# Down projection of a gated MLP as seven block products per pair of channel tiles

## The chip, the cores and the metric

The kernel runs on one core of a Trainium2 chip. A core has five engines with a queue each: TensorE (PE, with its weight loads as PEld), VectorE (DVE), ScalarE (ACT), GpSimd (POOL) and SyncE (SP), which here issues the transfers. The metric is the device time of one execution in microseconds.

## What is computed

```python
def _conv_ffn(x, w_up, conv_f_w, conv_f_b, w_down):
    h = _causal_depthwise_conv(x @ w_up, conv_f_w, conv_f_b)
    gate, val = h[..., :D_FF], h[..., D_FF:]
    return (jax.nn.silu(gate) * val) @ w_down

def reference(...):
    mix = _token_mixing(x, w_in, b_in, ...)
    x = _layernorm(DEEPNORM_ALPHA * x + mix, ln1_g, ln1_b)
    ffn = _conv_ffn(x, w_up, conv_f_w, conv_f_b, w_down)
    return _layernorm(DEEPNORM_ALPHA * x + ffn, ln2_g, ln2_b)
```

x is 1024 x 1024 in float32, D_FF is 2816, which is 22 tiles of 128 channels. The change lies in the product with w_down (2816 x 1024) and the last norm.

## The kernel before

Every float32 operand is split (`split`, L73 to L80) into a rounded high part, a cast on ACT at L75, and a low part, a subtract at L78 on POOL or DVE; three matmuls (high x high, high x low, low x high) make one product.

The program has four parts. The first computes the token mixing, the first norm and x1, which is kept in DRAM (`x1d`). The second runs the up units, one per tile f of 128 channels (`unit`, L702). A unit makes the gate tile `upg` and the value tile `upv`, 128 x 1024 each in PSUM, by a form of Strassen's scheme: seven products of 12 matmuls of 128x512 each in place of eight. Its weights are the row sums `sa` and `sb`, four DVE subtracts or adds (L692, L693, L696, L698 in `prep_unit`, for the unit after), split on ACT and POOL into `ws`, `wa`, `wb`, `wd`. Three DVE adds (L720, L721, L714) put the products' parts together in PSUM; the product t1 of the following unit goes to a half of the gate tile that L714 has read. Then the causal convolution of width 3 follows (`conv3`, ACT L633 and DVE L636), silu (L644), gate x value (L650 on DVE), and the result, `cg`, is stored to DRAM as `hd[f]` (L652).

The third is the down part. For each half of the rows (th) and each f, `down_prep` loads w_down[f] (`dr`) and half of hd[f] (`hr`), and splits them: `dh`, `dl` on ACT and POOL, `ho` on ACT and DVE. `down_step` then makes 6 matmuls for each of the four row tiles s of that half, into one 128x1024 PSUM tile `pd` per row tile, which collects over all f. The last, `finish`, adds ALPHA x1, takes the statistics (`rstd_row`, L98), and scales by g2 and b2: partly on ACT, POOL and DVE, row tile 7 in three pieces on DVE.

The order of the work is the order of the program for each queue, as the scheduler puts it; tiles of a pool wait until an older tile of the same tag is read to its end. The pools that matter are `raw` (3 buffers, loads to be split), `A` and `B` (16 each, split operands) and the PSUM pools `mm`, `un` and `dn`.

```python
            for n in range(2, 2 * NF):
                th, f = n // NF, n % NF
                ahead(n + 2)
                for s in range(4 * th, 4 * th + 4):
                    down_step(s, f)
```

## Time and profile before

| | |
|---|---|
| median of 3 runs | 997.17 us (995.89 to 997.5) |
| the profiled execution | 996.77 us |
| its span | 994.7 us, 2.07 us less than its time |
| PE busy | 964.9 us, 97% |
| DVE busy | 664.7 us, 67% |
| POOL busy | 534.9 us, 54% |
| ACT busy | 444.8 us, 45% |
| granted PE clock, mean | 0.993 |

The clock is a share of 2.4 GHz. Up to about 366 us the first part and the first unit run, from there to 741 us the other up units, to 985 us the down part, and then the end. "us from the start" counts from the start of the span. A row of the timeline gives start, length, engine, line, operation, output <- inputs, and in brackets the idle time before it with what released it. Numbers of buffers are left out of names, so `ws` stands for four split sums of a unit.

### The profile page before, as it was taken

To read this page: it belongs to the slowest core of one execution; us is meant where nothing else is said; L and a number is where in the kernel's file an instruction comes from. 1 tells how busy PE (TensorE), PEld (TensorE's weight loads), DVE (VectorE), ACT (ScalarE), POOL (GpSimd) and SP (SyncE) were. 2 spreads that over 40 slices of the span, in tenths; PEclk is the share of its full clock that TensorE was granted. 3 is DMA by queue.
4 is the path that set the end of the run, shared out by engine and by line. 5 is a ranking of instruction groups with operands and counts; after the bars stand their busy time and mean duration, and the time that the engine had idled before them with its cause. 6 is when DMAs were issued, how large, how long until landed. Compare 5 with 4: busy or idle time off the path is not lost.

```text
span 994.7 us, 11745 instructions
## 1 busy us (share of the span) xinstructions
PE 964.9 (97%) x4344; PEld 796.5 (80%) x4344; DVE 664.7 (67%) x890; ACT 444.8 (45%) x661; POOL 534.9 (54%) x341
## 2 busy tenths in 40 slices
PE   8999999999997799999999999999999999999996
PEld 6888888878885678888888888888877888888885
DVE  4699999987499995675675576567378344680007
ACT  5233864763634554454454444445455423343202
POOL 4245944775835974454544445445518744489402
PEclk9999999999998999999999999999999999999999
DMA  8111131321420233123123112212458744336102
GB/s 323 64 43 43 43 106 43 122 70 43 166 110 21 76 119 106 72 84 106 64 69 116 70 64 101 90 65 85 170 189 301 251 147 156 133 107 219 54 0 85
DMA packets 33177, 106.84 MB, mean 107 GB/s; under 512 B 3680, under 2 KB 4064, under 8 KB 33120
## 3 DMA queue, kind: packets, MB, share of 16 engines
q1 hardware_dynamic: 33120, 106.09, 30.3%
q8 instruction: 34, 0.56, 0.2%
q14 instruction: 23, 0.19, 0.1%
HBM read 86.16 MB, written 19.92 MB: 107 GB/s over the span
## 4 chain that ended last, share of the span: by engine, by line
PE 76%; DVE 17%; ACT 3%; DMA 2%; issue 1%; SPq 0%; POOL 0%; DVEq 0%; ACTq 0%
PE pd L828 23%; PE upv L624 20%; PE upg L624 15%; PE ps L215 8%; PE po L537 8%; DVE acc L263 6%; DMA xraw<-in_xT 1%; DVE cg L636 1%; DVE tq L758 1%; DVE tq L757 1%; DMA dr<-in_w_down 1%; DVE wol L78 1%; DVE ast L351 1%; DVE sa L693 1%; ACT vt L363 1%
## 5 line engine op out<-in xcount | busy, mean ns | idle before, releaser
L828 PE MATMUL pd<-dh,ho 128*128 128x512 f32 x688 | 213.4, 391 | 0.7 <-ACT dh L75 0.7
L78 POOL TENSOR_TENSOR dl<-dr,dh 128x1024 fp32r<-128x1024 f32 x44 | 109.8, 2507 | 87.8 <-ACT dh L75 87.8
L828 PEld LDWEIGHTS pd<-dh,ho 128*128 128x128 f32 x688 | 130.0, 189 | 28.0 <-ACT dh L75 1.1
L828 PE MATMUL pd<-dl,ho 128*128 128x512 f32 x344 | 134.7, 392 | 1.7 <-POOL dl L78 1.7
L263 DVE SCALAR_TENSOR_TENSOR acc<-ybin,cv,acc 128x512 f32<-128x512 f32 x196 | 134.2, 744 | 0.9 <-ACT acc L257 0.3
L78 DVE TENSOR_TENSOR ho<-hr,ho 128x512 fp32r<-128x512 f32 x44 | 77.8, 1790 | 61.2 <-ACT ho L75 61.2
L78 POOL TENSOR_TENSOR ws<-sb,ws 128x512 fp32r<-128x512 f32 x42 | 55.5, 1321 | 79.9 <-ACT ws L75 79.9
L75 ACT CAST dh<-dr 128x1024 fp32r<-128x1024 f32 x44 | 46.2, 1051 | 109.1 <-issue 50.3
L828 PEld LDWEIGHTS pd<-dl,ho 128*128 128x128 f32 x344 | 64.9, 189 | 15.7 <-POOL dl L78 2.2
L720 DVE TENSOR_TENSOR upv<-upv,pb 128x512 f32<-128x512 f32 x21 | 14.7, 698 | 78.9 <-PE upv L624 78.9
L78 POOL TENSOR_TENSOR ws<-sa,ws 128x512 fp32r<-128x512 f32 x42 | 58.9, 1405 | 6.1 <-ACT ws L75 6.1
L78 POOL TENSOR_TENSOR wa<-ur,wa 128x512 fp32r<-128x512 f32 x21 | 27.3, 1300 | 62.2 <-ACT wa L75 59.9
L636 DVE SCALAR_TENSOR_TENSOR cg<-upg,cv,cg 128x1023 f32<-128x1023 f32 (+4 forms) x46 | 56.6, 1230 | 5.9 <-ACT cg L633 5.3
L624 PE MATMUL upg<-b21h,wb 128*128 128x512 f32 x168 | 58.1, 391 | 1.6 <-POOL wb L78 1.2
L75 ACT CAST ws<-sb 128x512 fp32r<-128x512 f32 x42 | 26.1, 622 | 72.6 <-PE upv L624 70.3
L624 PE MATMUL upv<-b11h,wa 128*128 128x512 f32 x168 | 55.4, 391 | 2.1 <-DVE cg L636 2.1
L636 DVE SCALAR_TENSOR_TENSOR cv<-upv,cv,cv 128x1023 f32<-128x1023 f32 (+4 forms) x46 | 56.6, 1230 | 1.1 <-ACT cv L633 0.5
L624 PE MATMUL upv<-t2h,ws 128*128 128x512 f32 x168 | 55.3, 390 | 1.9 <-ACT pa L712 1.9
L624 PE MATMUL upg<-t1h,ws 128*128 128x512 f32 x168 | 55.3, 390 | 0.0
L624 PE MATMUL upv<-t4h,wd 128*128 128x512 f32 x168 | 55.3, 390 | 0.0
L624 PE MATMUL upv<-t3h,ws 128*128 128x512 f32 x168 | 55.1, 389 | 0.0
L624 PE MATMUL upg<-b22h,ws 128*128 128x512 f32 x168 | 55.1, 389 | 0.0
(411 smaller groups left out, 2340.0 us busy)
## 6 DMA issues: line engine op xcount, KB each, us to landing
ur<-in_w_up SPq DMA_DIRECT2D x44, 512.0 KB, 3.4
dr<-in_w_down SPq DMA_DIRECT2D x44, 512.0 KB, 3.9
hd<-cg SPq DMA_DIRECT2D x22, 512.0 KB, 2.9
hr<-hd SPq DMA_DIRECT2D x44, 256.0 KB, 3.2
wr<-in_w_in SPq DMA_DIRECT2D x14, 512.0 KB, 3.3
xres<-in_x SPq DMA_DIRECT2D x8, 512.0 KB, 3.9
wor<-in_w_out SPq DMA_DIRECT2D x8, 512.0 KB, 3.3
x1d<-xres SPq DMA_DIRECT2D x8, 512.0 KB, 2.6
```

Of the source, the lines that this page charges most:

```text
L75: nc.scalar.copy(hi, raw)
L78: lo_eng.tensor_tensor(out=lo, in0=raw, in1=hi.bitcast(F32), op=ALU.subtract)
L215: nc.tensor.matmul(ps[hf] if isinstance(ps, list) else ps[:, ts(hf, 512)], wt[:, ts(k, P)], xt(k, hf), start=first and k == 0, stop=(not f ...
L263: nc.vector.scalar_tensor_tensor(out=xs(0) if k == 0 else acc, in0=xs(k), scalar=w(k), in1=first if n == 0 else acc, op0=ALU.mult, op1=ALU ...
L351: nc.vector.bn_stats(st[:, n * 8 + g * 4 + c], tp[:, c])
L363: nc.scalar.activation(vc, vc, AF.Identity, bias=nb[:, i : i + 1], scale=r[:, i : i + 1])
L537: nc.tensor.matmul(po[:, ts(hf, 512)], a, b[:, ts(hf, 512)], start=first and i == 0, stop=last and i == 2)
L624: nc.tensor.matmul(out, w[a][:, ts(k, P)], x[b][k // 2][:, k % 2], start=first and k == 0 and i == 0, stop=last and k == 3 and i == 2, ski ...
L636: nc.vector.scalar_tensor_tensor(out=c[:, o:b], in0=ps[:, o - sh : b - sh], scalar=w(k), in1=c[:, o:b], op0=ALU.mult, op1=ALU.add,)
L693: tt(out=s2, in0=s1, in1=a11, op=ALU.subtract)
L720: v(out=w22, in0=x, in1=p5, op=ALU.add)
L828: nc.tensor.matmul(pd, hh[f][a][:, ts(s % 4, P)], wd[f][b][:, c0:c1], start=first and i == 0, stop=last and i == 2,)
```

## The change

Pairs of row tiles (p and p+4, p from 0 to 3), pairs of channel tiles (kp, 11 of them) and the two halves of the columns make 2 x 2 block products; each is now done with seven products in place of eight, of 3 matmuls each. The sums on the side of w_down do not depend on the hidden layer. `sum_prep(kp)` makes them in 11 of the up units: it loads two tiles of w_down (`dq0`, `dq1`), takes four DVE subtracts of 128x512 (L806 to L809), splits the result on ACT and POOL, and stores the four parts to DRAM. `wop_prep` loads these again in the down part, and splits the plain blocks. `hop_prep` loads parts of hd for a pair of row pairs, makes the sums with four DVE operations (L860 to L863) and splits all on ACT and POOL. `step` runs one product of a row pair, over one or two kp, into one half of one of two PSUM tiles, `xy0` and `xy1`; product 2 collects in a bank of its own (`z`) over all kp. After products 1, 6, 5, 3, 7 and 4 `accum` adds half a tile into x1 in SBUF (L927; the first time L930 with ALPHA). The order of products of a block is the string `seq`; the blocks take their kp in the order of `blocks`, so that the last four each finish one row pair. All row tiles but the last are then scaled on ACT and twice on POOL (L977 and L978).

```diff
-    ) as ap_, tc.tile_pool(name="b", bufs=16) as bp, tc.tile_pool(name="raw", bufs=3) as rawp, tc.tile_pool(
+    ) as ap_, tc.tile_pool(name="b", bufs=16) as bp, tc.tile_pool(name="raw", bufs=6) as rawp, tc.tile_pool(
...
-        def down_prep(th, f):
...
+        blocks = [
+            ((2, 3), (0,)), ((0, 1), (0, 1)), ((2, 3), (1, 2)), ((0, 1), (2, 3)), ((2, 3), (3, 4)), ((0, 1), (4, 5)),
+            ((2, 3), (5, 6)), ((0, 1), (6, 7)), ((2, 3), (7, 8)), ((0, 1), (8,)),
+        ] + [((p,), (9, 10)) for p in (0, 1, 2, 3)]
+
+        def sum_prep(kp):
+            w0, w1 = (load(w_down[2 * kp + i], f"dq{i}_{kp}") for i in range(2))
+            tt = nc.vector.tensor_tensor
+            b11, b12, b21, b22 = w0[:, 0:512], w0[:, 512:1024], w1[:, 0:512], w1[:, 512:1024]
+            tt(out=b11, in0=b12, in1=b11, op=ALU.subtract)
+            tt(out=b12, in0=b22, in1=b12, op=ALU.subtract)
+            tt(out=b22, in0=b22, in1=b11, op=ALU.subtract)
+            tt(out=b21, in0=b21, in1=b22, op=ALU.subtract)
+            wsum[kp] = []
+            for i, w in enumerate((w0, w1)):
+                hi = rawp.tile([P, 1024], F32R, tag="raw", name=f"dsh{i}_{kp}")
+                lo = w.bitcast(F32R)
+                split(w, hi, lo, nc.scalar, nc.gpsimd)
+                for q, t in (("h", hi), ("l", lo)):
+                    d = dp.tile([P, 1024], F32, name=f"ds{q}{i}_{kp}")
+                    nc.sync.dma_start(d, t.bitcast(F32))
+                    wsum[kp].append(d)
+
+        def wop_prep(kp):
+            ops = []
+            for i, d in enumerate(wsum[kp]):
+                t = A(F32R, f"ds{kp}_{i}")
+                nc.sync.dma_start(t.bitcast(F32), d)
+                ops.append((t[:, 0:512], t[:, 512:1024]))
+            b0 = rawp.tile([P, 512], F32, tag="raw", name=f"db0_{kp}")
+            nc.sync.dma_start(b0, w_down[2 * kp][:, 0:512])
+            b1 = load(w_down[2 * kp + 1], f"db1_{kp}")
+            h0 = A(F32R, f"dh0_{kp}", (P, 2, 512))
+            split(b0, h0[:, 0], h0[:, 1], nc.scalar, nc.gpsimd)
+            if kp % 3 == 2:
+                h1, l1 = (bp.tile([P, 1024], F32R, tag="B", name=f"d{q}1_{kp}") for q in "hl")
+            else:
+                h1, l1 = (wp.tile([P, 1024], F32R, tag=f"w{q}", name=f"d{q[0]}1_{kp}", bufs=2) for q in ("hi", "lo"))
+            split(b1, h1, l1, nc.scalar, nc.gpsimd)
+            (t1h, t3h), (t1l, t3l), (t4h, t2h), (t4l, t2l) = ops
+            wops[kp] = {
+                1: (h0[:, 0], h0[:, 1]), 2: (h1[:, 0:512], l1[:, 0:512]), 3: (h1[:, 512:1024], l1[:, 512:1024]),
+                5: (t1h, t1l), 6: (t2h, t2l), 7: (t3h, t3l), 4: (t4h, t4l),
+            }
+
+        def hop_prep(n):
+            pairs_, ks = blocks[n]
+            c0 = pairs_[0] // 2 * 256
+            nk = len(ks)
+            raw = []
+            for i in range(2):
+                t = rawp.tile([P, 2, nk, 256], F32, tag="raw", name=f"hr{n}_{i}")
+                for j, kp in enumerate(ks):
+                    nc.sync.dma_start(
+                        t[:, :, j], hd[2 * kp + i].rearrange("p (m c) -> p m c", m=2)[:, :, c0 : c0 + 256]
+                    )
+                raw.append(t)
+            a11, a21, a12, a22 = raw[0][:, 0], raw[0][:, 1], raw[1][:, 0], raw[1][:, 1]
+            ss = [rawp.tile([P, 2, nk, 256], F32, tag="raw", name=f"hs{n}_{i}") for i in range(2)]
+            s1, s2, s4 = ss[0][:, 0], ss[0][:, 1], ss[1][:, 0]
+            tt = nc.vector.tensor_tensor
+            tt(out=s1, in0=a21, in1=a22, op=ALU.add)
+            tt(out=a21, in0=a11, in1=a21, op=ALU.subtract)
+            tt(out=s2, in0=s1, in1=a11, op=ALU.subtract)
+            tt(out=s4, in0=a12, in1=s2, op=ALU.subtract)
+            op = lambda q: bp.tile([P, 2, nk, 256], F32R, tag="B", name=f"ho{n}_{q}")
+            o = [op(i) for i in range(7)]
+            split(raw[0], o[0], o[1], nc.scalar, nc.gpsimd)
+            split(raw[1], o[2], o[3], nc.scalar, nc.gpsimd)
+            split(ss[0], o[4], o[5], nc.scalar, nc.gpsimd)
+            split(s4, o[6][:, 0], o[6][:, 1], nc.scalar, nc.gpsimd)
...
+                for kp in range(NP):
+                    if 2 + kp * 9 // 5 == f:
+                        sum_prep(kp)
                 if f == NF - 1:
-                    for n in range(3):
-                        down_prep(0, n)
+                    down_prep(0)
+                    for t in (2, 6, 3, 7, 0, 4, 1, 5):
+                        load_x1(t)
+                    down_prep(1)
                 value_tile(f, gate_tile(f))
...
-            def down_mm(pd, s, f, c0, c1, first, last):
...
+            def down_prod(bank, n, ks, q, j, first, last):
+                for i, kp in enumerate(ks):
+                    for c, (a, b) in enumerate(((0, 0), (0, 1), (1, 0))):
+                        nc.tensor.matmul(
+                            bank, hops[n][q][a][:, i, ts(j, P)], wops[kp][q][b],
+                            start=first and i == 0 and c == 0, stop=last and i == len(ks) - 1 and c == 2,
+                            skip_group_check=True,
+                        )
+
+            def accum(bank, s, hf, out=None):
+                dst = xr_[s][:, ts(hf, 512)]
+                if (s, hf) in touched:
+                    nc.vector.tensor_tensor(out=dst if out is None else out, in0=bank, in1=dst, op=ALU.add)
+                else:
+                    touched.add((s, hf))
+                    nc.vector.scalar_tensor_tensor(out=dst, in0=dst, scalar=ALPHA, in1=bank, op0=ALU.mult, op1=ALU.add)
+
+            def step(n, q, i):
+                pairs_, ks = blocks[n]
+                p = pairs_[i]
+                b = xy[p % 2]
+                x, y = b[:, 0:512], b[:, 512:1024]
+                j = p % 2
+                end = n == len(blocks) - 1
+                if q == 2:
+                    if p not in zs:
+                        zs[p] = dnp.tile([P, 512], F32, tag="dn", name=f"z{p}")
+                    fin = ks[-1] == NP - 1
+                    down_prod(zs[p], n, ks, 2, j, p not in zused, fin)
+                    zused.add(p)
+                    if fin:
+                        accum(zs[p], p, 0)
+                    return
+                down_prod(y if q in (5, 3) else x, n, ks, q, j, q in (1, 5), q in (4, 3))
+                if q == 1:
+                    accum(x, p, 0)
+                if q == 6:
+                    accum(x, p, 1)
+                if q == 5:
+                    accum(y, p + 4, 1)
+                if q == 3:
+                    accum(y, p, 1)
+                if q == 7:
+                    accum(x, p + 4, 1, y if end else None)
+                if q == 4:
+                    accum(x, p + 4, 0, x if end else None)
+
+            def finish(s):
+                t = xr_[s]
+                mv = stats(s, [t[:, ts(hf, 512)] for hf in range(2)])
+                r, nb = rstd_row(mv, f"l2_{s}", True)
+                cuts = [(0, 512), (512, 1024)] if s == 3 else [(0, 1024)]
+                for a, b in cuts:
+                    nc.scalar.activation(t[:, a:b], t[:, a:b], AF.Identity, bias=nb, scale=r)
+                    nc.gpsimd.tensor_tensor(out=t[:, a:b], in0=t[:, a:b], in1=g2[:, a:b], op=ALU.mult)
+                    nc.gpsimd.tensor_tensor(out=t[:, a:b], in0=t[:, a:b], in1=b2[:, a:b], op=ALU.add)
+                    nc.sync.dma_start(out[s][:, a:b], t[:, a:b])
...
+            for n, (pairs_, ks) in enumerate(blocks):
+                if n + 1 < len(blocks):
+                    down_prep(n + 1)
+                if len(pairs_) == 2:
+                    seq = "1a1b5a5b6a6b7a7b3a3b4a4b2a2b" if n == 0 else "1a1b2a2b6a6b5a5b7a7b3a4a4b3b"
+                else:
+                    seq = "1a5a6a3a7a2a4a"
+                for q, i in zip(seq[0::2], seq[1::2]):
+                    step(n, int(q), "ab".index(i))
+                if ks[-1] == NP - 1:
+                    p = pairs_[0]
+                    finish(p)
+                    if n < len(blocks) - 1:
+                        finish(p + 4)
                     else:
+                        finish_last(p + 4, [xy[p % 2][:, ts(hf, 512)] for hf in range(2)])
 
 
 def kernel(**inputs):
```

The order of DVE's instructions beside up unit 11, before. The names carry the unit's number; `upv11` is its value tile, `sa14` the row sums made for a later unit, `upg12` the gate tile that the next t1 waits for (its L714 is the ninth row):

```order
L720 TENSOR_TENSOR upv11_4342<-upv11_4342,pb11_4348 128x512
L692 TENSOR_TENSOR sa14_4713<-ur14_1_4619 128x512
L721 TENSOR_TENSOR upg11_4341<-upg11_4341,pa11_4347 128x512
L693 TENSOR_TENSOR sa14_4713<-sa14_4713,ur14_0_4617 128x512
L696 TENSOR_TENSOR sb14_4714<-ur14_0_4617,ur14_1_4619 128x512
L698 TENSOR_TENSOR sb14_4714<-ur14_0_4617,sa14_4713 128x512
L636 SCALAR_TENSOR_TENSOR cg11_4466<-upg11_4341,cv_84,cg11_4466 128x1023
L636 SCALAR_TENSOR_TENSOR cg11_4466<-upg11_4341,cv_84,cg11_4466 128x1022
L714 TENSOR_TENSOR upg12_4478<-upg12_4478,pa12_4484 128x512
L636 SCALAR_TENSOR_TENSOR cv11_4471<-upv11_4342,cv_84,cv11_4471 128x1023
L636 SCALAR_TENSOR_TENSOR cv11_4471<-upv11_4342,cv_84,cv11_4471 128x1022
```

and after, where pair 5 has its sums:

```order
L806 TENSOR_TENSOR dq0_5_4576<-dq0_5_4576 128x512
L720 TENSOR_TENSOR upv11_4452<-upv11_4452,pb11_4458 128x512
L807 TENSOR_TENSOR dq0_5_4576<-dq1_5_4578,dq0_5_4576 128x512
L808 TENSOR_TENSOR dq1_5_4578<-dq1_5_4578,dq0_5_4576 128x512
L692 TENSOR_TENSOR sa14_4867<-ur14_1_4773 128x512
L809 TENSOR_TENSOR dq1_5_4578<-dq1_5_4578 128x512
L721 TENSOR_TENSOR upg11_4451<-upg11_4451,pa11_4457 128x512
L693 TENSOR_TENSOR sa14_4867<-sa14_4867,ur14_0_4771 128x512
L696 TENSOR_TENSOR sb14_4868<-ur14_0_4771,ur14_1_4773 128x512
L698 TENSOR_TENSOR sb14_4868<-ur14_0_4771,sa14_4867 128x512
L636 SCALAR_TENSOR_TENSOR cg11_4598<-upg11_4451,cv_84,cg11_4598 128x1023
L714 TENSOR_TENSOR upg12_4610<-upg12_4610,pa12_4616 128x512
```

The first `dq0` subtract (L806) stands ahead of L720, and the other three between L720 and L721. L714 stands behind one of the two conv adds in place of both.

POOL's order at the same place, after. Before, `ws4`, `wd`, `wb` and `wa` follow one another there without the `dq` rows:

```order
L78 TENSOR_TENSOR ws412_4570<-sb12_4550,ws412_4570 128x512
L78 TENSOR_TENSOR dq0_5_4576<-dq0_5_4576,dsh0_5_4584 128x1024
L78 TENSOR_TENSOR wd12_4573<-ur12_1_4455,wd12_4573 128x512
L78 TENSOR_TENSOR wb13_4713<-ur13_0_4612,wb13_4713 128x512
L78 TENSOR_TENSOR dq1_5_4578<-dq1_5_4578,dsh1_5_4591 128x1024
L78 TENSOR_TENSOR wa13_4710<-ur13_0_4612,wa13_4710 128x512
```

The two 128x1024 `dq` subtracts stand ahead of `wd` and of `wa`.

DVE in a full block of the down part, after (`hs5` are the row sums for the block that follows). Before, DVE had there only one `ho` subtract per half of a hidden tile, with nobody on PE's side waiting between:

```order
L927 TENSOR_TENSOR x1r0_6099<-xy0_6173,x1r0_6099 128x512
L927 TENSOR_TENSOR x1r1_6103<-xy1_6174,x1r1_6103 128x512
L860 TENSOR_TENSOR hs5_0_6684<-hr5_0_6678,hr5_1_6681 128x512
L927 TENSOR_TENSOR x1r0_6099<-xy0_6173,x1r0_6099 128x512
L861 TENSOR_TENSOR hr5_0_6678<-hr5_0_6678 128x512
L862 TENSOR_TENSOR hs5_0_6684<-hs5_0_6684,hr5_0_6678 128x512
L927 TENSOR_TENSOR x1r1_6103<-xy1_6174,x1r1_6103 128x512
L863 TENSOR_TENSOR hs5_1_6685<-hr5_1_6681,hs5_0_6684 128x512
L927 TENSOR_TENSOR x1r4_6101<-xy0_6173,x1r4_6101 128x512
L927 TENSOR_TENSOR x1r5_6105<-xy1_6174,x1r5_6105 128x512
L927 TENSOR_TENSOR x1r4_6101<-xy0_6173,x1r4_6101 128x512
L927 TENSOR_TENSOR x1r5_6105<-xy1_6174,x1r5_6105 128x512
```

Each L927 frees a half of `xy0` or `xy1` for PE's next product on that tile, and the four sums for the next block stand between them. Over the down part PE has 924 matmuls of 128x512, in place of the work of 1056.

## Rows read from the trace of the kernel before

**Rows 1.** windows: span time, then busy us and matmul count of each engine, granted clock, DMA
```profile
core 0: us, PE busy (x) PEld busy (x) DVE busy (x) ACT busy (x) POOL busy (x), PEclk, DMA share, GB/s
366.00:724.00 358.00, 357.44 (x1578) 295.71 (x1577) 220.17 (x219) 165.59 (x244) 178.44 (x132) 1.00 0.26 92
...
748.00:870.00 122.00, 122.00 (x533) 100.85 (x532) 65.51 (x40) 45.53 (x58) 69.65 (x28) 0.99 0.56 195
870.00:985.00 115.00, 115.00 (x519) 95.70 (x518) 38.88 (x64) 27.89 (x35) 59.60 (x24) 1.00 0.26 92
```

**Rows 2.** the chain that ended last, in order of time: the row of the down products
```profile
747.21 232.66 PE pd L828 x1018
```

**Rows 3.** DVE and POOL timelines inside one up unit: start us, us, instruction
```profile
585.93 0.70 DVE L720 TENSOR_TENSOR upv<-upv,pb 128x512 f32<-128x512 f32 x1 [4.21 <-PE upv L624]
...
591.07 1.77 DVE L696 TENSOR_TENSOR sb<-ur,ur 128x512 f32<-128x512 f32 x1 [1.19 <-POOL wd L78]
592.76 0.68 DVE L698 TENSOR_TENSOR sb<-ur,sa 128x512 f32<-128x512 f32 x1
593.36 2.59 DVE L636 SCALAR_TENSOR_TENSOR cg<-upg,cv,cg 128x1023 f32<-128x1023 f32 x2
595.87 0.69 DVE L714 TENSOR_TENSOR upg<-upg,pa 128x512 f32<-128x512 f32 x1
...
599.16 1.60 DVE L650 TENSOR_TENSOR cg<-cg,cv 128x1024 f32<-128x1024 f32 x1
...
589.33 1.71 POOL L78 TENSOR_TENSOR wd<-ur,wd 128x512 fp32r<-128x512 f32 x1 [1.42 <-ACT wd L75]
590.98 1.31 POOL L78 TENSOR_TENSOR wb<-ur,wb 128x512 fp32r<-128x512 f32 x1
```

**Rows 4.** SP and PE timelines of the same unit: a store's issue, and the product t1
```profile
581.75 0.33 SPq L652 DMA_DIRECT2D hd<-cg  x1
...
597.00 0.39 PE L624 MATMUL upg<-t1h,ws 128*128 128x512 f32 x1
```

**Rows 5.** the page's costliest groups: what a split, a cast and a PSUM add cost, mean ns
```profile
L78 POOL TENSOR_TENSOR dl<-dr,dh 128x1024 fp32r<-128x1024 f32 x44 | 109.8, 2507 | 87.8 <-ACT dh L75 87.8
...
L78 DVE TENSOR_TENSOR ho<-hr,ho 128x512 fp32r<-128x512 f32 x44 | 77.8, 1790 | 61.2 <-ACT ho L75 61.2
...
L75 ACT CAST dh<-dr 128x1024 fp32r<-128x1024 f32 x44 | 46.2, 1051 | 109.1 <-issue 50.3
...
L720 DVE TENSOR_TENSOR upv<-upv,pb 128x512 f32<-128x512 f32 x21 | 14.7, 698 | 78.9 <-PE upv L624 78.9
```

**Rows 6.** DVE and POOL timelines in the down part, both engines at two-input subtracts
```profile
787.36 1.15 DVE L78 TENSOR_TENSOR ho<-hr,ho 128x512 fp32r<-128x512 f32 x1 [5.72 <-ACT ho L75]
790.91 2.78 DVE L78 TENSOR_TENSOR ho<-hr,ho 128x512 fp32r<-128x512 f32 x1 [2.40 <-ACT ho L75]
...
785.56 7.57 POOL L78 TENSOR_TENSOR dl<-dr,dh 128x1024 fp32r<-128x1024 f32 x3 [1.67 <-ACT dh L75]
```

**Rows 7.** windows around the start of the down part and in an earlier stretch with idle PE
```profile
340.00:350.00 10.00, 6.49 (x27) 4.50 (x27) 9.96 (x13) 7.11 (x12) 10.00 (x8) 1.00 0.29 105
...
742.00:748.00 6.00, 3.57 (x14) 2.31 (x14) 5.32 (x7) 5.70 (x7) 3.04 (x2) 1.00 0.94 336
748.00:754.00 6.00, 6.00 (x21) 4.77 (x20) 5.90 (x4) 3.88 (x7) 6.00 (x3) 0.72 0.97 360
```

**Rows 8.** the page's DMA issues: KB each, median us to landing
```profile
dr<-in_w_down SPq DMA_DIRECT2D x44, 512.0 KB, 3.9
...
hr<-hd SPq DMA_DIRECT2D x44, 256.0 KB, 3.2
```

**Rows 9.** timeline after the last matmul
```profile
985.16 0.28 PE L828 MATMUL pe7c<-dh,ho 128*128 128x256 f32 x1
...
991.20 0.48 DVE L898 SCALAR_TENSOR_TENSOR x1r<-pe7c,rowl,b2row 128x256 f32<-128x256 f32 x1
```

**Rows 10.** DVE's groups by line, 950 us to the end: mean ns of a statistics instruction
```profile
L869 DVE BATCH_NORM_STATS2 fst<-x1r 128x6 f32<-128x512 f32 x4 | 2.6, 686 | 0.1
```

More of the change, by code (lines that the diff above doesn't have):

```diff
@@ L807, in build, with down_prep, load_x1 @@
+        def down_prep(n):
+            for kp in blocks[n][1]:
+                if kp not in wops:
+                    wop_prep(kp)
+            key = (blocks[n][0][0] // 2, blocks[n][1])
+            if key not in hset:
+                hset[key] = hop_prep(n)
+            hops[n] = hset[key]
+        def load_x1(s):
+            xr_[s] = xt(f"x1r{s}")
+            nc.sync.dma_start(xr_[s], x1d[s])
         with tc.tile_pool(name="un", bufs=2, space=PSUM) as unp:
@@ L823, in build @@
             nc.sync.dma_start(b2, rows[4:5].broadcast_to([P, 1024]))
-            pds = {}
-            def down_mm(pd, s, f, c0, c1, first, last):
-                for i, (a, b) in enumerate(((0, 0), (0, 1), (1, 0))):
-                    nc.tensor.matmul(
-                        pd, hh[f][a][:, ts(s % 4, P)], wd[f][b][:, c0:c1], start=first and i == 0, stop=last and i == 2,
-                    )
-            xr_ = {}
-            def load_x1(s):
-                t = xp.tile([P, PAD + S], F32, tag="x", name=f"x1r{s}")[:, 0:1024]
-                nc.sync.dma_start(t, x1d[s])
-                xr_[s] = t
@@ L839, in open_ @@
[L839 to L855 removed]
+            xy = [mmp.tile([P, 1024], F32, tag="mm", name=f"xy{i}") for i in range(2)]
@@ new lines, in stats @@
+            def stats(s, srcs):
+                st = stp.tile([P, 2, 6], F32, tag="fst", name=f"fst{s}")
+                mv = stp.tile([P, 2], F32, tag="lmv", name=f"fmv{s}")
+                for hf in range(2):
+                    nc.vector.bn_stats(st[:, hf], srcs[hf])
+                nc.vector.bn_aggr(mv, st)
+                return mv
+            def finish(s):
[8 more added lines that the diff above has]
+                    nc.sync.dma_start(out[s][:, a:b], t[:, a:b])
@@ L856, in finish, with finish_last @@
+            def finish_last(s, srcs):
+                t = xr_[s]
+                mv = stats(s, srcs)
+                r, _ = rstd_row(mv, f"l2_{s}", False)
+                for hf in range(2):
+                    nc.vector.scalar_tensor_tensor(
+                        out=srcs[hf], in0=srcs[hf], scalar=mv[:, 0:1], in1=g2[:, ts(hf, 512)], op0=ALU.subtract,
+                        op1=ALU.mult,
+                    )
+                for hf in range(2):
                     nc.vector.scalar_tensor_tensor(
-                        out=t, in0=t, scalar=ALPHA, in1=pd, op0=ALU.mult, op1=ALU.add, accum_out=sm[:, 0:1]
+                        out=t[:, ts(hf, 512)], in0=srcs[hf], scalar=r, in1=b2[:, ts(hf, 512)], op0=ALU.mult, op1=ALU.add
@@ L880, in finish @@
-                if s < 7:
-                    if s >= 4:
-                        nc.scalar.activation(t, pd if s == 6 else t, AF.Copy, scale=r)
-                    nc.gpsimd.tensor_tensor(out=t, in0=t, in1=b2, op=ALU.add)
-                    nc.sync.dma_start(out[s], t)
-                    return
-                for i, (ph, (a, b)) in enumerate(zip(pd, cuts)):
-                    with tc.issue_after(last_dve[0]):
-                        nc.vector.tensor_tensor(out=ph, in0=ph, in1=t[:, a:b], op=ALU.add)
-                    for c in range(a // 256, b // 256):
-                        nc.vector.bn_stats(st[:, c], ph[:, c * 256 - a : c * 256 - a + 256])
```

122 lines of the change are left out of this document (11 added, 111 removed).

## The prediction

> **What bounds the kernel now.** I read the windows by stage first. In the up units PE is busy for 357.44 of 358.00 us, and in the down part for all of its two windows [rows 1]: a saving of TensorE work there is a saving of time, as long as nobody else becomes late. One matmul costs 357.44 / 1578 = 0.2265 us [rows 1]. In the same stretch DVE is busy for 220 of 358 us and POOL for 178, so each of the 19.0-us up units (84 matmuls) has about 7 us of idle DVE and 9.5 us of idle POOL. The chain of waits says the same: PE alone carries the end for 232.66 us of the down part [rows 2].
>
> The next view is the timeline of DVE and POOL in one unit, since idle time only helps if it lies where the new work goes. The last row to read is L714, the add that frees the gate's PSUM tile for product t1. It ends at 596.56 [rows 3], and t1 starts at 597.00 [rows 4]. The slack is 0.44 us. Ahead of L714 on DVE stand the row sums L692 to L698 and a pair of conv adds of 2.59 us [rows 3]. These two-input SBUF subtracts have two prices. L698 took 0.68 us; L696, beside a busy POOL, 1.77, and POOL's own wd took 1.71 where wb took 1.31 [rows 3]. In the down part it is plainer: POOL runs three 128x1024 subtracts in 7.57 us, DVE's subtract takes 2.78 us against them, and DVE's mean over 44 is 1.79 [rows 5, 6]. The two engines alternate. An add with one input in PSUM is not stretched (L720, mean 0.698 [rows 5]).
>
> **The change part by part.** The bound for calling a difference real is 0.2%, 2 us. The sum starts from the profiled execution, 996.77 us (span 994.7 and 2.07 outside it), 0.40 below the median of 997.17.
>
> *TensorE work.* Before, the down part has 22 channel tiles x 8 row tiles x 2 halves x 3 = 1056 matmuls of 128x512 (the last in narrower pieces). After it has 11 pairs x 7 products x 4 row pairs x 3 = 924. 132 x 0.2265 = **-29.9 us**. Removed too are 44 DVE subtracts (77.8 us busy [rows 5]), but they wait in PE's shadow and give nothing back by themselves.
>
> *Sums in the up units.* Eleven units get 4 DVE subtracts, 2 casts (1.05 us), 2 POOL subtracts (2.4 to 2.5 us), 2 loads and 4 stores [rows 5]. By totals they fit: 4 x 0.68 = 2.7 of 7 idle us on DVE, 5 of 9.5 on POOL, 2.1 on ACT; the DMA share is 0.26 in this stretch [rows 1], and 6 x 0.5 MB x 11 = 33 MB about doubles it, which I cost at nothing. By order they do not fit as well. The load of dq0 follows the store of the unit before, issued at 581.75 [rows 4]; with 3.9 us to land [rows 8] and its turn in the queue it is there at about 586.2. L806 now stands ahead of L720, which ran at 585.93 [rows 3]: L806 to 586.9, L720 to 587.6. L807, L808, L692 and L809 then run to 590.3. POOL's dq0 subtract needs dq0 cast after L807, so it starts at about the same moment and L809 has a fair chance to be first. L721 to 591.0; L693 waits for the 2.4-us dq0, to 593.3; L696 alternates with wd, to 595.0; L698 with wb, to 596.4; one conv add (half of 2.59) to 597.7; L714 to 598.4, and with two hand-overs of some 0.3 us t1 starts at 599.0 in place of 597.0. The stall is **2.0 us**. If L698 falls behind dq1 instead, it is 2.4 more, 4.4. If no subtract collides, L698 ends by 592.9, L714 by 594.9, and the stall is 0. I take 2.0, for the order says that L698 is due before POOL's wb is through. This pattern holds in six units (pairs 3, 4, 5, 7, 8, 9). Pairs 0 to 2 have their L806 to L809 in a denser place; I give them the same 2.0. Pairs 6 and 10 have them where L714 has no queue behind them, 0.5 each. 9 x 2.0 + 1 = **+19 us** (0 to 9 x 4.4 + 1 = 41).
>
> *Start of the down part.* Today PE is busy for 3.57 of the 6 us from 742 and then runs at clock 0.72 for 6 us, 21 matmuls for 28 [rows 7]: 2.4 + 7 x 0.2265 = 4.0 us lost. After, the first add into x1 stands on DVE behind the convs of unit 21 (2.59 twice, then the product of 1.6 [rows 3]), some 7.6 us. The first block then has 12 adds (8.4 us) and 4 subtracts (2.7 to 7), and ends near 20 us for 42 matmuls that need 9.5. That is 10.5 lost in place of 4.0, **+7 us** (2 to 11).
>
> *Full blocks.* Eight blocks hold 84 matmuls, 19.0 us. Each product of 6 (1.36 us) writes half of one of two PSUM tiles, and the next product on that tile waits for the add of 0.70. The rest of the path is about 0.3 (a matmul lasts 0.39 and the next starts 0.2265 later [rows 4]), so the slack is some 0.35 us. Four times per block an `hs` subtract stands between two adds: 4 x (0.70 - 0.35) = 1.4 us, if it is not stretched. Stretched as L696 is, it is 4 x 1.4 = 5.7. POOL has 12 us of work per block, so both happen; but the z products between some adds give 1.36 us more cover, so I take the low value. **8 x 1.4 = +11 us** (4 to 45). Transfers hide: 41 MB in place of 33 MB at 0.56 and 0.26 of the engines [rows 1], but the subtract waits for its 256-KB transfers, 3.2 us each [rows 8], issued only when POOL frees a buffer; that lies in the upper end. The half block 9 has products of 0.68 us, shorter than the add path of 1.0: about 6 x 0.38 = **+2 us**.
>
> *End.* Today the last matmul ends at 985.44 and the span 9.3 us later [rows 9]. After, both row pairs 2 and 3 finish at once. From the last matmul DVE has two adds, five bn_stats (0.69 [rows 10]), three sets of small operations and two multiplies of 0.75 in one queue: about 10 us until row tile 6 may be scaled. Then ACT 1.1 us, and POOL does g for 6, b for 2, g for 3, b for 6, b for 3 (2.4 each, tile 3 in halves), 12.4 us in order; with the 3.0 us from the last operation to the end today [rows 9] that makes 26 us. **+16 us** (5, if only DVE's own row tile 7 counted, to 18).
>
> Sum: 996.8 - 29.9 + 19 + 7 + 11 + 2 + 16 = **1022 us**.
>
> **What the skill says.** The traces show that the engines alternate, with either one waiting: DVE's 2.78 and POOL's 1.71 [rows 3, 6]. The Trainium skill, "SBUF — State Buffer", section "Who interferes with whom", says that an instruction of VectorE with two SBUF inputs and one of GpSimd that reads SBUF exclude each other for the whole instruction, and that issue order decides who waits. By that rule it speaks against this change, and the up term depends on a race: 19 us where DVE is first, up to 41 where POOL's dq1 is. The trace agrees (2.78 us is 0.68 and most of a 2.4-us POOL operation) and does not tell who wins.
>
> The clock: PE lost 1.6 us to a low clock after 2.4 idle us, yet a stretch with 3.5 idle of 10 us ran at 1.00 [rows 7]. The Trainium skill, "TensorE: Matmul & The Clock Gate", Part 1, says that the throttled clock is the default state and activity releases it. By that each of nine stalls could cost 1.6 us again, +14 and 1036; by the second row none does, 1022. I keep the second.
>
> **The rivals.**
> 1. *The cover holds, and it gets faster.* The subtracts fall into DVE's idle stretches before POOL's new work starts, so L714 stays ahead of t1. For it: 7 idle us per unit, a four-us hole before L720 [rows 3], and most L692 to L698 unstretched today. Then: up +1, start +3, blocks +3, half block +1, end +8: 996.8 - 29.9 + 16 = 983. It is decided by whether L714 ends before PE asks for t1. Chance 0.28.
> 2. *POOL wins the races.* dq1 gets ahead of L698 in all nine units (+41 for +19), and the low clock follows each stall (+14): 1022 + 22 + 14 = 1058; with one of the two, 1036 to 1044. For it: POOL is in mid-operation when DVE's subtracts arrive in the down part [rows 6]. Chance 0.24.
> 3. *The blocks are bound by their adds*: 5.7 for 1.4 us in half of the eight, +17: 1039. It is in the same upper range; chance 0.08.
> 4. *Gain and loss cancel* within 2 us: 0.05. That the products are not fewer is no rival: the order has 924.
>
> **How the numbers follow.** The forecast, 1010 to 1032, has 0.35. Above it lies 0.32, below it 0.28 in the faster case and 0.05 at no change. The range leaves out about one in ten at either side: from 978 (rival 1 with an end of +3) to 1056. Faster 0.28, same 0.05, slower 0.67.
>
> **What would show it.** Right: about 924 matmuls and some 209 busy us in the down part; PE waiting for DVE's L714 in units with sums, 2 us each, with L693 to L698 near 1.7 us; two-input subtracts beside POOL above 1.5 us; first products of the down part waiting for DVE; over 20 us between the last matmul and the end, on POOL's L977 and L978. Wrong: PE still fully busy from 366 to 724, a down part of 210 to 220 us, or an end of about 10 us; each strikes its own term.

## The result, and the profile after

The changed kernel takes 1074.41 us (median of 4 runs, 1070.68 to 1078.9) against 996.53 for the kernel before (median of 4): ratio 1.0779, 95% interval 1.0737 to 1.082. It is slower, as forecast, but by 78 us in place of 25, and outside the range of 978 to 1056.

The span grew from 994.7 to 1069.3 us. The windows by stage tell where; first of the kernel before (up units from 366 us to the last up matmul, down part to the last matmul, end), then of the changed kernel (columns as in [rows 1]):

```profile
366.00:741.29 375.29, 374.73 (x1654) 310.04 (x1653) 233.66 (x233) 173.93 (x256) 180.83 (x133) 1.00 0.27 95
741.29:985.59 244.30, 241.72 (x1069) 199.69 (x1067) 111.01 (x110) 80.02 (x100) 132.29 (x53) 0.99 0.43 149
985.59:994.70 9.11, 0.00 (x0) 0.00 (x0) 5.87 (x17) 0.86 (x2) 2.34 (x1) 0.76 0.30 115
```

```profile
366.00:785.59 419.59, 391.65 (x1659) 317.59 (x1658) 300.09 (x272) 190.63 (x273) 248.05 (x154) 0.97 0.47 169
785.59:1046.59 261.00, 226.23 (x924) 175.90 (x924) 157.85 (x241) 68.55 (x82) 153.32 (x78) 0.96 0.48 162
1046.59:1069.30 22.71, 0.00 (x0) 0.00 (x0) 8.39 (x28) 4.67 (x7) 16.39 (x9) 0.58 0.35 139
```

| stage | forecast | measured |
|---|---|---|
| up units | +19 | 419.6 - 375.3 = +44.3 |
| down part | -29.9 + 7 + 11 + 2 = -10 | 261.0 - 244.3 = +16.7 |
| end | +16 | 22.7 - 9.1 = +13.6 |

The 924 matmuls came. In the up units PE sat idle for 27.9 us, and its matmuls were busy 16 us longer than as many took before (1659 in 391.65 us, against 1654 in 374.73). In the down part 924 matmuls at 0.2265 would be 209.3 us; they were busy for 226.2, and 34.8 us were idle. PE's waits in the whole changed kernel (engine, tile and line that waited, what for, us, times, longest):

```profile
PE upg L624 <- DVE upg L714: 20.9, 7, 3.4
PE xy L918 <- DVE x1r L927: 20.1, 14, 3.5
PE upv L624 <- ACT pa L712: 11.5, 6, 4.5
PE xy L918 <- ACT ho L75: 7.7, 1, 7.7
PE xy L918 <- DVE x1r L930: 4.4, 2, 4.0
```

Of the waits for L712 the longest, 4.5 us, lies ahead of 366 us, so in the up units L714 has 20.9 us and L712 7.0.

The timeline of DVE in one sum unit, then POOL's two new subtracts and PE's t1, where [rows 3, 4] showed the unit before:

```profile
528.56 0.69 DVE L806 TENSOR_TENSOR dq<-dq 128x512 f32<-128x512 f32 x1 [5.96 <-DMA dq<-in_w_down]
529.17 0.69 DVE L720 TENSOR_TENSOR upv<-upv,pb 128x512 f32<-128x512 f32 x1
...
532.19 2.89 DVE L809 TENSOR_TENSOR dq<-dq 128x512 f32<-128x512 f32 x1
535.00 0.69 DVE L721 TENSOR_TENSOR upg<-upg,pa 128x512 f32<-128x512 f32 x1
...
538.41 2.86 DVE L698 TENSOR_TENSOR sb<-ur,sa 128x512 f32<-128x512 f32 x1
541.20 1.27 DVE L636 SCALAR_TENSOR_TENSOR cg<-upg,cv,cg 128x1023 f32<-128x1023 f32 x1
542.39 0.68 DVE L714 TENSOR_TENSOR upg<-upg,pa 128x512 f32<-128x512 f32 x1
...
532.11 2.42 POOL L78 TENSOR_TENSOR dq<-dq,dsh 128x1024 fp32r<-128x1024 f32 x1 [1.71 <-ACT dsh L75]
537.90 2.82 POOL L78 TENSOR_TENSOR dq<-dq,dsh 128x1024 fp32r<-128x1024 f32 x1
...
543.13 0.50 PE L624 MATMUL upg<-t1h,ws 128*128 128x512 f32 x1 [3.41 <-DVE upg L714]
```

This is the chain of the prediction with both races lost: L809 takes 2.89 us beside `dq0`, L698 2.86 beside `dq1`, and t1 is 3.41 us late. The first row has something else: DVE had nothing to do for 5.96 us, because L806 stood at the head of its queue and the load was not there. In the unit before, DVE idled there too, 4.21 us until PE had L720's input [rows 3], and L720 is only about 0.5 us later against t1 (10.55 us ahead of the moment when PE asked for t1, 543.13 - 3.41, for 597.00 - 585.93 = 11.07). What the late load took is the use of this hole: the four subtracts ran behind it, among the row sums and beside POOL.

### The profile page after: what moved, and what is told of

The parts are those of the page before. It is cut to its first block, busy times and chain, and to the rows that moved or that the text cites. A ratio compares the mean times of both kernels' runs of the same rounds, so it can differ in the third digit from the quotient of the medians.

```text
span 1069.3 us, 11986 instructions
## 1 busy us (share of the span) xinstructions
PE 967.5 (90%) x4200; PEld 781.5 (73%) x4200; DVE 777.9 (73%) x1071; ACT 453.4 (42%) x664; POOL 635.2 (59%) x394
## 4 chain that ended last, share of the span: by engine, by line
PE 51%; DVE 22%; DMA 9%; issue 7%; POOL 6%; ACT 2%; SPq 1%; POOLq 0%; DVEq 0%; ACTq 0%
PE ps L215 15%; PE upv L624 9%; PE xy L918 8%; PE po L537 8%; PE upg L624 7%; DMA dq<-in_w_down 4%; DMA hr<-hd 3%; POOL ho L78 2%; DVE cg L636 2%; DVE dq L809 2%; DVE sb L698 2%; DVE cv L636 2%; DVE x1r L927 1%; PE z L918 1%; POOL ws L78 1%
## 5 line engine op out<-in xcount | busy, mean ns | idle before, releaser
L918 PE MATMUL xy<-ds,ho 128*128 128x512 f32 x528 | 134.2, 401 | 18.4 <-DVE x1r L927 15.5
L927 DVE TENSOR_TENSOR x1r<-xy,x1r 128x512 f32<-128x512 f32 x126 | 86.4, 689 | 68.7 <-PE xy L918 68.5
L918 PEld LDWEIGHTS xy<-ds,ho 128*128 128x128 f32 x528 | 98.9, 191 | 48.0 <-DVE x1r L927 23.0
L78 POOL TENSOR_TENSOR ho<-hr,ho 128x1024 fp32r<-128x1024 f32 (+1 forms) x24 | 54.7, 2291 | 60.6 <-ACT ho L75 60.6
L918 PE MATMUL xy<-dh,ho 128*128 128x512 f32 x220 | 67.4, 413 | 16.4 <-ACT ho L75 7.7
L624 PE MATMUL upg<-t1h,ws 128*128 128x512 f32 x168 | 61.0, 427 | 20.9 <-DVE upg L714 20.9
L78 POOL TENSOR_TENSOR dq<-dq,dsh 128x1024 fp32r<-128x1024 f32 x22 | 56.1, 2550 | 27.0 <-ACT dsh L75 23.3
L75 ACT CAST ho<-hr 128x1024 fp32r<-128x1024 f32 (+1 forms) x24 | 23.1, 978 | 99.0 <-PE xy L918 70.2
L918 PEld LDWEIGHTS xy<-dh,ho 128*128 128x128 f32 x220 | 43.4, 199 | 28.8 <-ACT ho L75 8.1
L624 PEld LDWEIGHTS upg<-t1h,ws 128*128 128x128 f32 x168 | 34.5, 205 | 31.5 <-DVE upg L714 23.8
```

The source lines that it names most:

```text
L75: nc.scalar.copy(hi, raw)
L78: lo_eng.tensor_tensor(out=lo, in0=raw, in1=hi.bitcast(F32), op=ALU.subtract)
L624: nc.tensor.matmul(out, w[a][:, ts(k, P)], x[b][k // 2][:, k % 2], start=first and k == 0 and i == 0, stop=last and k == 3 and i == 2, ski ...
L918: nc.tensor.matmul(bank, hops[n][q][a][:, i, ts(j, P)], wops[kp][q][b], start=first and i == 0 and c == 0, stop=last and i == len(ks) - 1 ...
L927: nc.vector.tensor_tensor(out=dst if out is None else out, in0=bank, in1=dst, op=ALU.add)
```

## The experiments

Each run stands against the kernel before on the same chip; where a part is left out, its expectation says so. "Up" is the time from 366 us to the last up matmul, as above. The same up code took 419.6 to 424.6 us in five kernels whose edits lie behind it (one has a seventh raw buffer), so 5 us there say nothing. Nor are all kernels equally far at 366 us: 1654 up matmuls are left in the kernel before, 1659 in the changed one, 1670 in e3 and 1679 in f3, at 0.2265 us each. Most of these kernels ran twice (f4 and f7 four times), and their times lie up to 8 us apart (d3). Line numbers move with the edits.

**Sums without DVE's part (e1), without POOL's part (e2), without both (e4).** e1 drops the first four lines of the diff, e2 changes the rest, e4 does both.

```diff
-            tt(out=b11, in0=b12, in1=b11, op=ALU.subtract)
-            tt(out=b12, in0=b22, in1=b12, op=ALU.subtract)
-            tt(out=b22, in0=b22, in1=b11, op=ALU.subtract)
-            tt(out=b21, in0=b21, in1=b22, op=ALU.subtract)
...
-                split(w, hi, lo, nc.scalar, nc.gpsimd)
-                for q, t in (("h", hi), ("l", lo)):
+                nc.scalar.copy(hi, w)
+                for q, t in (("h", hi), ("l", hi)):
```

> Leaves out the four DVE subtracts on w_down in the up units; loads, casts, POOL subtracts and stores stay. In the changed kernel the up units take 42 us more than before: PE idles 28 us of it, mostly until L714, and runs 15 us slower at a low granted clock after the idle stretches. Theory A (the subtracts stand ahead of L714 on DVE and wait for POOL): idle in the up units falls to under 5 us and the clock loss with it, total about 1036. Rival B (POOL's two extra subtracts alone hold up the row sums L692 to L698): about half stays, total about 1055. Rival C (loads and stores): the stalls stay, about 1074.

> Leaves out POOL's two subtracts per sum unit (the low part is stored as a copy of the high part); the four DVE subtracts stay. Theory A with the shared access as cause (L809 took 2.9 us behind POOL's dq0, L698 2.9 behind dq1): both fall to 0.7, L714 is in time, idle under 5 us, total about 1036. Rival D (four more instructions on DVE are enough by themselves, 2.8 us, whoever else runs): stalls of 2 us and more stay in the sum units, total 1055 or more. Rival C: about 1074.

> Leaves out both the four DVE subtracts and the two POOL subtracts of each sum unit; loads, the two casts on ACT and four stores stay. Alone, the first left 418 us for the up units after 366 us and the second 408, against 420 in the changed kernel and 375 before. Theory I (DVE and POOL share one access: a sum unit asks 21.4 us of two-input work of both in 19.0 us, 18.6 without the DVE part, 16.6 without the POOL part): 13.8 us are asked here, so the up units take under 382 us and the total is 1030 to 1038. Rival J (work that waits for the late load of w_down stands ahead of the unit's own chain, now the casts ahead of the copies on ACT that PE waits for): over 10 us of stalls stay, up units 390 or more, total 1045 or more.

Measured: e1 1065.23 us (up 418.3), e2 1054.05 (up 407.8), e4 1037.70 (up 386.8). Theory A fell: without the DVE subtracts the up units gained 1.3 us, and without POOL's 11.8, each far from the 1036 that it gave. The stalls moved. In e1 the cast of `dq` on ACT now waits for the load, with the unit's own convolution queued behind it, so that DVE lacks its input (timelines of ACT, then DVE):

```profile
527.07 2.22 ACT L75 CAST dsh<-dq 128x1024 fp32r<-128x1024 f32 x2 [2.64 <-DMA dq<-in_w_down]
...
531.95 2.60 DVE L636 SCALAR_TENSOR_TENSOR cg<-upg,cv,cg 128x1023 f32<-128x1023 f32 x2 [4.19 <-ACT cg L633]
...
538.37 0.50 PE L624 MATMUL upg<-t1h,ws 128*128 128x512 f32 x1 [2.87 <-DVE upg L714]
```

In e2 the second cast waits for L809 and holds the copy `pa` that product t2 needs; PE waits 16.0 us for L712 in its up units. e4 kept 386.8, between the 382 of theory I and the 390 of rival J.

**Loads one unit earlier (e3), the same with casts alone (e6), one sum unit in place of eleven (e5).** The first part of the diff is that of e3 and e6, the second that of e5.

```diff
                 load_unit(f + 1)
+                for kp in range(NP):
+                    if 2 + kp * 9 // 5 == f + 1:
+                        sum_load(kp)
                 unit(f)
...
+                        if kp == 0:
                             sum_prep(kp)
+                        else:
+                            wsum[kp] = wsum[0]
```

> The two loads of each sum unit are put one unit earlier in the program; nothing is left out. Theory J (late loads at the heads of the queues): the up units fall to 390 us or less, total 1045 or less. Theory I (two-input work on DVE and POOL does not fit a unit): less than 10 us gained, up units 410 or more, total 1064 to 1078.

> Leaves out ten of the eleven sum units (all products of the down part use the sums of pair 0), with their loads, DVE and POOL subtracts, casts and stores. The up units take 419.6 us after 366 us in the changed kernel, 393.5 with early loads, 386.8 with loads and casts alone, 375.3 before. Theory J (the late loads and what waits for them are all of it): up units 375 to 381 us, total 1029 to 1037. Rival N (something else of the change, as the six buffers for raw tiles, holds up the up units): over 385 us, total 1040 or more.

> Early loads, and both the DVE and the POOL subtracts of the sum units left out, so that only loads, casts on ACT and stores stay. Late loads with this little work leave 386.8 us for the up units (e4_casts_only), early loads with all of the work 393.5 (e3_early_load), one sum unit alone 379.5 (e5_one_sum). If what stays with early loads is the two-input work on DVE and POOL: 379 to 383 us. If loads, casts or stores hold it: 388 or more.

Measured: e3 1042.39 (up 393.5), e5 1028.27 (379.5), e6 1023.40 (378.4). The up units of e3, e4 and e6 (windows):

```profile
366.00:759.49 393.49, 383.70 (x1670) 312.62 (x1668) 276.29 (x273) 196.43 (x277) 249.11 (x158) 1.00 0.49 178
```

```profile
366.00:752.79 386.79, 378.75 (x1658) 309.95 (x1656) 233.29 (x229) 192.13 (x274) 181.87 (x133) 1.00 0.50 185
```

```profile
366.00:744.39 378.39, 377.18 (x1662) 311.38 (x1660) 234.43 (x233) 195.04 (x276) 182.55 (x134) 1.00 0.50 185
```

The two loads moved one unit ahead in the program, with all of the work kept, give back 26 of the 44 us in the up units, and 32 in all. What DVE waited for at the sums, first in the changed kernel, then in e3 (the view of the tile `dq`: lengths as ns min/median/max, then DVE's idle time ahead of these instructions):

```profile
L809 DVE TENSOR_TENSOR dq<-dq x11: 692/2884/2894, 384.0 to 766.2; 128x512 f32<-128x512 f32 x11
its engine sat idle before it (us, times) until:
  DMA dq<-in_w_down: 43.0, 14
```

```profile
L814 DVE TENSOR_TENSOR dq<-dq x9: 673/679/1781, 418.0 to 715.3; 128x512 f32<-128x512 f32 x9
its engine sat idle before it (us, times) until:
  DMA dq<-in_w_down: 0.8, 2
```

43 us of waiting at the head of DVE's queue became 0.8, and the order that comes with data in time put L814 (L809 of the changed kernel) mostly beside no POOL operation; the subtracts of two pairs now run ahead of 366 us (x9 for x11). Theory J is the nearer one: the total kept to its 1045 or less, the up units missed its 390 by 3.5 us. e5 rules out rival N: with one sum unit 379.5 us stay, 4 above the kernel before. e6 against e3 shows that the 15 us that stay with early loads are the subtracts on DVE and POOL: 378.4 without them, 1 us from what one sum unit leaves.

The late loads do not cost their 26 us alone. Late against early, they cost 419.6 - 393.5 = 26 us with the subtracts and 386.8 - 378.4 = 8 us with the casts alone; the subtracts cost 15 us with early loads and 419.6 - 386.8 = 33 with late ones. Some 18 us need both: in the unit shown, late data put the subtracts where the unit's own chain and POOL are busy. How much is the wait at the head of a queue, and how much the changed order beside POOL, no run shows apart.

**The down part: sums on ACT as copies (d2), sums later (d4), one more buffer (d1).** d2 puts three copies of a block, `nc.scalar.copy(s1, a22)` and so on, for L860 to L863; d1 has `bufs=7` for the raw pool. In d4 `hop_prep` only loads; the sums and splits of the next block are called after the seventh step of a block, and the sums stay behind the last add on DVE:

```diff
-                hset[key] = hop_prep(n)
+                hop_prep(n)
...
+                with tc.issue_after(last_acc[0]):
+                    sums()
...
                     step(n, int(q), "ab".index(i))
+                    if m == min(6, len(seq) // 2 - 1) and 1 < n + 1 < len(blocks):
+                        down_sums(n + 1)
```

> Replaces the four DVE sums of a down block (L860 to L863) by three copies of a block on ACT into the same buffers, so transfers, buffers, splits and the order of buffers stay, but nothing on DVE waits for the transfers ahead of PE's adds. Theory E (an L860 that waits for its 256-KB transfers stands ahead of the adds that PE waits for): the waits for L927 between 850 and 1000 us, some 15 us of idle, fall under 4, and total falls by 10 to 20 us. Rival F (the add path of 1 us against products of 1.36 us): the waits stay, total within 5 us of 1074.

> The four DVE sums for the next block stand behind the fifth to seventh add of a block in place of the third; nothing is left out. Theory E (L860 waits at the head of DVE's queue for transfers that land some 5 us into the block, with PE's adds behind it): the waits for adds between 850 and 1000 us fall by half or more, down part 235 to 250 us in place of 261, total 1048 to 1064. Rival K (the splits behind the sums then come late, and PE waits for them at the next block): total 1070 or more.

> One more buffer in the pool for raw loads (7 for 6). Theory G (the transfers of the next block's hidden tiles are issued late because all six buffers are held until POOL has split them): L852 is issued earlier, the waits for L860's data shrink by 1 to 2 us per block, total 8 to 15 us less. Rival H (the transfers wait for the program's order on SP or for the stores): total within 4 us of 1074.

Measured: d2 1039.92 us (down part 225.8 in place of 261.0), d4 1059.22 (245.3), d1 1076.26 (264.7). PE's waits between 850 and 1000 us, of the changed kernel, d2 and d4:

```profile
PE xy L918 <- DVE x1r L927: 16.2, 9, 3.5
```

```profile
PE xy L916 <- DVE x1r L925: 1.2, 1, 1.2
```

```profile
PE xy L938 <- DVE x1r L951: 2.7, 3, 1.0
```

Theory E holds, and rival F falls: with nothing late ahead of them, the adds keep up with products of 1.36 us. d2's total fell by 34 us, more than the 10 to 20 of theory E, since it leaves out the sums' work as well and PE was busy for 216.65 us in place of 226.23. In the changed kernel DVE sat idle in front of L860 until the transfers of `hr` had landed, with the adds behind it:

```profile
885.14 0.69 DVE L927 TENSOR_TENSOR x1r<-xy,x1r 128x512 f32<-128x512 f32 x1 [0.67 <-PE xy L918]
887.48 0.69 DVE L860 TENSOR_TENSOR hs<-hr,hr 128x512 f32<-128x512 f32 x1 [1.65 <-DMA hr<-hd]
...
890.21 1.28 DVE L927 TENSOR_TENSOR x1r<-xy,x1r 128x512 f32<-128x512 f32 x2
```

d4 keeps the same sums and loses most of the waits by its order alone. d1 gained nothing: with one more buffer DVE still waited 14.6 us for these transfers between 840 and 1000 us, for 16.8 in the changed kernel.

**The end (d3), and the three together (f1).** d3 replaces ACT's scaling and the POOL operations of row tile 3 by `scalar_tensor_tensor` on DVE, in halves, as row tile 7 has them. f1 is e3, d4 and d3.

> Row tile 3 is scaled by two DVE operations per half, as row tile 7 is, in place of ACT and four POOL multiplies and adds; nothing is left out. Theory L (POOL's queue of multiplies and adds sets the end, 22.7 us after the last matmul): the end comes 16 to 18.5 us after the last matmul, total 4 to 6 us less. Rival M (DVE's chain of statistics sets it): within 1.5 us of 22.7, or later.

> Early loads, the sums of a block behind its fifth add, and row tile 3 scaled on DVE, all three together; nothing is left out. If the three act in separate parts of the program, the gains add: 32 + 15 + 3, total 1020 to 1030. If the earlier end of the up units only moves work into a start of the down part that waits for its transfers, 10 us of it are lost: 1030 to 1040.

Measured: d3 1071.04 us, from times of 1066.99 and 1075.10, too far apart to tell a gain of 3; its end was 20.8 us for 22.7: less gained than theory L asked, more than rival M. DVE now had the multiplies of row tile 3 in its queue, and row tile 6 was scaled 10.1 us after the last matmul in place of 6.7. f1 1021.71: the gains add, 53 us in all, and the full blocks ran without a stall (windows):

```profile
777.00:840.00 63.00, 63.00 (x274) 51.10 (x275) 33.38 (x51) 16.86 (x20) 44.40 (x23) 1.00 0.63 213
840.00:900.00 60.00, 60.00 (x264) 48.84 (x262) 32.49 (x50) 15.43 (x18) 38.97 (x19) 1.00 0.60 204
```

**Sum units one unit later (f2), x1 loaded later (f3).** f2 has `3 + kp * 9 // 5` for `2 + ...`; f3 moves the loop of `load_x1` behind `down_prep(1)`.

> As f1_three, and every sum unit one up unit later (the first beside unit 3 in place of 2). If the first sum unit lies in the crowded stretch around 350 us, where PE waits 4 to 5 us for ACT's copy at L712, 3 to 6 us less than f1_three. If only the number of sum units matters: within 2 us of f1_three.

> As f1_three, with the eight loads of x1 (4 MB) behind the loads of the second block in place of ahead of them. If the start of the down part is bound by transfers (share 0.93 to 0.99 between 760 and 793 us), the first waits of PE for ACT's cast of the hidden tiles shrink: 3 to 8 us less than f1_three. If the first adds then wait for x1: within 2 us or slower.

Measured: f2 1032.42, f3 1026.04. Neither helped. f2 came out 11 us slower, which neither reading had: its wait at L712 near 345 us stayed at 5.2 us, so the first sum unit is not its cause, and the start of the down part then waited 9.5 us for a cast. f3's down part took 242.2 us against 242.1; its up units are 4 us longer because 20 more matmuls were left at 366 us.

**What was still open (f4, f5, f6, f7).** f4 loads for block 12 and calls its sums in block 10, and puts the norm's DVE work on row tile 3 behind that on row tile 6; f7 is f4 with f1's norm; f5 is f4 with `bufs=7`; f6 is f5 with loads two units ahead.

> As f1_three, with the sums of the last hidden tiles (block 12) two blocks earlier, and in the last norm the DVE work of row tile 3 behind that of row tile 6, whose multiplies on POOL run in halves; nothing is left out. Theory E again: the 7.4 us that PE waits for ACT's cast near 973 us, whose sums stand on DVE behind the statistics of the row tiles finished before, vanish, and the end comes 13 to 15 us after the last matmul in place of 17.6: total 1009 to 1014. If the buffers for operands are what is late there: 1016 or more.

> As f4_last_block, with seven raw buffers for six. If the buffers still hold back the early loads in the up units (391.5 us after 366 us in f1_three, 375.3 before): up units 380 to 386 us, 5 us or more less than f4_last_block. If what is left there is the work itself on DVE and POOL: within 3 us of f4_last_block.

> As f5_seven, with the loads of the sums two units ahead. If the loads are still late one unit ahead: up units 385 us or less. If they are not, and what is left is the work on DVE and POOL and where the order puts it: within 4 us of f5_seven, either side.

> As f4_last_block, with the last norm as in f1_three again. f4's end came 21.8 us after the last matmul in place of 17.6. If its new order of row tiles 3 and 6 did that (halves on POOL beside DVE's multiplies of tile 3): the end comes 17 to 19 us after the last matmul, total 1012 to 1016. If the shorter down part did it, since POOL still has the multiplies of the row tiles before: 21 us or more again, total 1017 or more.

Measured: f4 1018.10 us (ratio 1.0208, 1.0163 to 1.0253), f7 1019.86, f5 1033.17, f6 1035.68. In f4 the wait of 7.4 us was gone and the down part at 235.4 us, but the end grew to 21.8 us, so the total missed its 1009 to 1014; f7's end was 20.7, so little of this is f4's order and most comes with the shorter down part. POOL itself stood idle for 4.01 us ahead of its last multiply in f7; the chain stood on DVE, whose 128x1 operations L105, L106 and L109 took 1.41, 1.79 and 1.81 us while POOL still worked on the row tiles before. With f5 the up units took 404.6 us, against both readings of its expectation; f6, with 406.5, is within 4 us of f5, its second reading. The views of `dq` tell why: with another buffer the scheduler set another order, in which DVE stands waiting for the loads again (f5, f6; the same row has 2.6 us in f4, and f1 has none):

```profile
  DMA dq<-in_w_down: 20.5, 9
```

```profile
  DMA dq<-in_w_down: 14.0, 10
```

So it is not enough that a load stands early in the program; the order must not put work on it ahead of its landing. No version beat the kernel before; the best is 2% slower.

## Why the prediction was right or wrong

**TensorE work, -29.9: right** in its count, 924 matmuls; but the sum priced each at 0.2265 us, and in the down part they took 226.23 / 924 = 0.245. **End, +16: right in kind and size**, +13.6 (its own terms, 10 + 1.1 + 12.4 + 3.0 less 9.3, make +17). POOL's queue closes it, in the order forecast (the chain that ended last):

```profile
1053.28 1.25 ACT x1r L976
...
1054.60 2.34 POOL x1r L977
1056.94 2.29 POOL x1r L978
1059.23 2.44 POOL x1r L977 x2
1061.67 2.30 POOL x1r L978
```

Row tile 6 was scaled 6.7 us after the last matmul in place of "about 10".

**Sums in the up units, +19: the wait for L714 came in its size; the clock and a second wait, both put at nothing, made it +44.** PE waited 20.9 us for L714, close to the 19 of the sum, but in 7 stalls of 3.0 us and not 9 of 2.0, so the closeness is in part luck. In the unit shown two steps of the chain failed: with "L809 has a fair chance to be first" it took 9.9 us from L806 to the end of L696 in place of 8.8, and with "L698 is due before POOL's wb is through" L698 took 2.86 us beside `dq1` in place of 1.4. The unit lost 3.4 and not 2.0 us. "It is there at about 586.2", 4.5 us after the store's issue, was 5.9 (issue 522.63, L806 528.56), but the store was issued earlier against t1, so L806 started 11.2 us ahead of the moment when PE asked for t1, and the forecast had 10.8.

The step that failed at the largest price is the clock. "I keep the second", no loss, was the wrong row to keep: the same matmuls were busy 16 us longer, which is most of the 25 us missing here. The mean granted clock, 0.97 of 419.6 us, stands for 12.6 of them, an estimate from that row; the rest is not explained. Next is the wait for L712, 7.0 us, which had no term: I asked only what the new work does on DVE to L714, and not what a cast that waits for late data holds up on ACT. The totals of idle time per engine, which spoke for the faster rival, told nothing of it. e1 shows how misleading one chain is: it took the chain's subtracts away and the stall came by ACT. e3 and e4 show what the stalls come from: without the late loads 26 of the 44 us go, without the subtracts 33.

After one stall of 3.4 us the granted clock was 0.60 and 0.83 for two windows of 6 us, means of the two levels, 1.2 and 2.4 GHz; after another it stayed at 1.00, 2.4 GHz. Some 3 us ahead of the first stall PE had waited 0.97 us, ahead of the second 0.30 us; what decides is not shown (windows of the changed kernel):

```profile
490.00:496.00 6.00, 3.46 (x14) 2.19 (x13) 6.00 (x5) 4.60 (x6) 6.00 (x4) 1.00 0.44 175
496.00:502.00 6.00, 4.17 (x10) 3.30 (x11) 5.86 (x6) 2.05 (x3) 3.15 (x3) 0.60 0.47 175
502.00:508.00 6.00, 6.00 (x24) 4.82 (x23) 1.54 (x1) 2.21 (x4) 2.49 (x3) 0.83 0.48 175
...
536.00:542.00 6.00, 3.42 (x14) 2.18 (x12) 6.00 (x4) 3.88 (x6) 6.00 (x4) 1.00 0.52 206
542.00:548.00 6.00, 4.87 (x21) 4.05 (x22) 5.86 (x6) 3.06 (x5) 3.16 (x4) 1.00 0.42 143
```

In the down part matmuls were busy 17 us longer (226.2 - 209.3), of which the mean granted clock, 0.96 of 261.0 us, stands for 10, by the same estimate. The reading of the Trainium skill, "TensorE: Matmul & The Clock Gate", Part 1, which gave +14, was the nearer one; the second rows show that not every stall pays. In e6, without long stalls, the up units ran at 1.00 and 377.18 busy us.

**Full blocks, +11: right place, wrong price.** "4 x (0.70 - 0.35) = 1.4 us" took the subtracts to be ready. They waited for their transfers: PE waited 20.1 us for L927, for 11 + 2 in the sum, and of the 16.2 between 850 and 1000 us all but 1.2 went in d2 and all but 2.7 in d4, which keeps the sums. The sentence that put this "in the upper end" was the main term among the waits. **Start, +7: near in size, wrong in cause.** The prediction lost 10.5 us to adds on DVE. The first adds cost 4.4; ahead of them PE waited 7.7 us for a cast of the hidden tile. The timelines of ACT and DVE show a late load again, `db`, at the head of ACT's queue with the convolution of the last unit behind it, and then L860, at 2.45 us, ahead of the rest of that convolution:

```profile
784.92 0.62 ACT L75 CAST dh<-db 128x512 fp32r<-128x512 f32 x1 [6.88 <-DMA db<-in_w_down]
...
786.68 1.28 DVE L636 SCALAR_TENSOR_TENSOR cg<-upg,cv,cg 128x1023 f32<-128x1023 f32 x1 [3.08 <-ACT cg L633]
787.88 2.45 DVE L860 TENSOR_TENSOR hs<-hr,hr 128x256 f32<-128x256 f32 x1
...
792.58 1.12 ACT L75 CAST ho<-hr 128x512 fp32r<-128x512 f32 x2
```

Rival 2, "POOL wins the races" with the clock after each stall, 1058, had the right mechanisms in the up units and was the nearest, there with +55 for 44.3; that its total came close owes something to the down part, where it had -10 for +16.7. Rival 3's wait for the adds was there too, but late transfers made it, not the stretch beside POOL. I had them as alternatives with small chances; they came together, and the range, built from one at a time, was too narrow above.
